# A linear-attention stage whose TensorE work is issued in the order of the program

## The chip, the core and the metric

The kernel runs on one core of a Trainium2 chip. The metric is the device time of one execution in microseconds (us). A core has a tensor engine for matrix products (TensorE, PE in the profile, with its weight loads as PEld), a vector engine (VectorE, DVE), a scalar engine (ScalarE, ACT), a general engine (GpSimd, POOL) and a queue engine (SyncE, SP) that mostly issues DMAs. Each engine takes its instructions in one fixed order; engines wait for each other through semaphores. Matrix products land in PSUM, a memory of eight banks; all else lives in SBUF.

## The reference

One inference step of a two-layer decoder, in float32: 512 new prompt tokens and 8 decode samples, model width 1024. Layer 0 mixes tokens with sliding-window attention, layer 1 with gated linear attention (GLA); after each comes an up-projection, a short convolution, a gate and a down-projection (ConvFFN, width 2816), and each sublayer ends in a LayerNorm of its sum with the input. The change lies in the GLA. For each of four heads:

```python
# log_a = log_sigmoid((x @ w_a1) @ w_a2 + b_a) / 16      rank-16 decay, from x
def step(S, inp):                       # one chunk of the sequence, state S is 128 x 256
    qc, kc, vc, lc = inp
    b = jnp.cumsum(lc, axis=2)
    q_in, k_in = qc * jnp.exp(b), kc * jnp.exp(-b)
    att = jnp.where(causal, q_in @ k_in.T, 0.0)
    o = att @ vc + q_in @ S
    S_new = exp(b_last) * S + (kc * jnp.exp(b_last - b)).T @ vc
o = o * rsqrt(mean(o ** 2) + eps) * norm_g * silu(g)     # then @ w_o
```

The eight samples do one such step each, from a state that is read from memory and written back.

## The kernel before

**Tiling.** Activations are kept transposed, 128 features by tokens, in two groups: a has 256 prompt tokens, b has 256 and the 8 samples. A weight matrix is cut into units of 128 output features. `plan` lists the units, `order` deals them out to the groups: within a phase (attention, out-projection, FFN, GLA, out-projection, FFN) group b follows group a by four or five units. The GLA phase has 25 units: the rank projection (`gla_rank`), and for each head q, k, v0, v1, g0, g1 (`gla_q`, `gla_k`, `gla_v`, `gla_g`).

**Main products.** `product` multiplies a unit with a group: float32 is split into a high and a low part, and each of eight slices takes three matmuls (L173 to L175), 24 in all, into one of four PSUM banks `accp`. The rank projection takes two per slice (L671, L672), 16 in all.

**Small products.** What is left are full float32 products and transposes: the decay of a head (L681), the scores k by q (L730), transposes of k and v (L750 to L752), the state update and the output (L767 `up`, L775 q by the scaled state `sp`, L778 the scores by v), the same for the samples (L814 to L816, then L827 and L828), and the transposes of the normed output for the gate (L866, L868). They use four more banks, by tag: two `sc`, one `tp`, one `pv` (`mtile`). A tile of a tag waits until the tag's earlier tile has been read.

**Order.** Each unit's work is a Python generator. `run` calls one unit per step, a slot; `yield n` puts the rest of the generator off by n slots, and `due` runs what is due after the unit's own product. The heap takes them by slot and then by the order in which they were put in. So in the program a unit's product comes first and the small products of earlier units behind it. The LayerNorm that ends the FFN of layer 0 is such a generator too (`ln_end`): for group b it resumes one slot after the last FFN unit, that is behind the rank projection of group a, with two sums over the features on PE (L256), then DVE, ACT and POOL steps that deliver eight chunks of 128 features (L296 to L301).

The program is not the order of issue. The framework (`TileContext`, with a timeline estimate) lists instructions that are ready, prefers those earlier in the program, and fixes an order for each engine when the kernel is built. It may issue a later product before an earlier one. `manual_schedule(engines=...)`, used at the kernel's start for SP alone (L323), keeps the named engines in program order for what is traced inside it.

**The samples.** `gla_sample` is started by group b's v1 unit. It transposes the samples' v, copies it to a DRAM tile and reads it back broadcast to 128 partitions; multiplies q with eight states (L827, 32 columns each); norms the result; and updates the states one pair per slot, with DVE and ACT operations pinned in program order (L844, L845).

Of the kernel before, what the change touches and what calls it, by code (L numbers as in the profile page):

```python
# [11 lines left out]
F32 = mybir.dt.float32  # L12
F32R = mybir.dt.float32r
I32 = mybir.dt.int32
AF = mybir.ActivationFunctionType
# [5 lines left out]
P = 128  # L21
# [70 lines left out]
class Net:  # L92
# [624 lines left out]
    def gla_k(self, g, u, h):  # L717
        nc, n = self.nc, g.n
        ps = self.product(g, u, g.xh, g.xl)
        yield 1  # L720
        g.k = self.gp.tile([P, n], F32, name=f"k_{g.name}")
        nc.vector.tensor_tensor(g.k, ps, g.em, op=ALU.mult)
        if g.i:
            g.kraw = self.gp.tile([P, NS], F32, name="kraw", bufs=2)
            nc.vector.tensor_copy(g.kraw, ps[:, 256:])
        yield 1
        att = self.mtile("sc")
        for b in range(2):
            bs = slice(b * P, (b + 1) * P)
            nc.tensor.matmul(att[:, bs], g.k[:, bs], g.q[:, bs], start=True, stop=True)  # L730
        g.att = self.attm[self.attm_i % 2]
        self.attm_i += 1
        nc.vector.copy_predicated(g.att, self.causal.unsqueeze(1).broadcast_to([P, 2, P]), att[:, :256].rearrange("p (b t) -> p b t", b=2))

    def gla_v(self, g, u, h, i):
        nc, n = self.nc, g.n
        ps = self.product(g, u, g.xh, g.xl)
        vt = self.gp.tile([P, n], F32, name=f"v{i}_{g.name}")
        nc.scalar.copy(vt, ps)
        if i == 0:  # L740
            g.v0 = vt
            return
        yield 1
        q, k, v0, v1, att, eb = g.q, g.k, g.v0, vt, g.att, g.eb
        ctx = dict(q=q, k=k, v0=v0, v1=v1, ep=g.ep, kraw=g.kraw) if g.i else None
        vks = []
        for b in range(2):
            bs = slice(b * P, (b + 1) * P)
            mp = self.mtile("tp")
            nc.tensor.transpose(mp[:, 0:P], k[:, bs], self.ident)  # L750
            nc.tensor.transpose(mp[:, P:2 * P], v0[:, bs], self.ident)
            nc.tensor.transpose(mp[:, 2 * P:3 * P], v1[:, bs], self.ident)  # L752
            vk = self.gp.tile([P, 3 * P], F32, name="vk", bufs=2)
            nc.scalar.copy(vk, mp[:, :3 * P])
            vks.append(vk)
        if g.i:
            self.spawn(self.gla_sample(g, h, **ctx), 0)
        yield 1
        o = self.mtile("pv")
        small = self.gp.tile([P, 8], F32, name="gsmall", bufs=2)  # L760
        st = self.tst[:, h]
        for b in range(2):
            bs = slice(b * P, (b + 1) * P)
            ob = o[:, b * 256:(b + 1) * 256]
            first = g.i == 0 and b == 0
            up = self.mtile("sc")[:, :256]
            nc.tensor.matmul(up, vks[b][:, 0:P], vks[b][:, P:], start=True, stop=True)  # L767
            if first:
                nc.vector.tensor_copy(st, up)
            else:  # L770
                f = self.gp.tile([P, 1], F32, name="f", bufs=2)
                nc.vector.tensor_tensor(f, self.ebl[:, h:h + 1], eb[:, 2 * b:2 * b + 1], op=ALU.mult)
                sp = self.gp.tile([P, 256], F32, name="sp", bufs=2)
                nc.vector.tensor_scalar(sp, st, f, None, op0=ALU.mult)
                nc.tensor.matmul(ob, q[:, bs], sp, start=True, stop=False)  # L775
                nc.vector.tensor_tensor(st, up, sp, op=ALU.add)
            nc.vector.tensor_copy(self.ebl[:, h:h + 1], eb[:, 2 * b + 1:2 * b + 2])
            nc.tensor.matmul(ob, att[:, b], vks[b][:, P:], start=first, stop=True)  # L778
        if g.i:
            so = self.gp.tile([P, 256], F32, name="sp", bufs=2)  # L780
            nc.vector.tensor_scalar(so, st, self.ebl[:, h:h + 1], None, op0=ALU.mult)
            nc.scalar.dma_start(out=self.O["gla_p"][h], in_=so)
        on = self.gp.tile([P, 512], F32, name="on", bufs=2)
        for b in range(2):
            ob = o[:, b * 256:(b + 1) * 256]
            nc.scalar.activation(on[:, b * 256:(b + 1) * 256], ob, AF.Square, accum_out=small[:, b:b + 1])
        rs = self.rms(small[:, 0:8], P, 2)
        for b in range(2):
            bs = slice(b * 256, (b + 1) * 256)
            nc.scalar.activation(on[:, bs], o[:, bs], AF.Copy, scale=rs[:, b:b + 1])  # L790
        g.on = on
# [13 lines left out]
    def gla_sample(self, g, h, q, k, v0, v1, ep, kraw):  # L805
# [22 lines left out]
        nc.tensor.matmul(os_, self.qkd, vs[:, :256], start=False, stop=True)  # L828
        small = self.gp.tile([P, 4], F32, name="ssmall")
        jk = self.gp.tile([P, 256], F32, name="sp", bufs=2)  # L830
        nc.scalar.activation(jk, os_, AF.Square, accum_out=small[:, 0:1])
        rs = self.rms(small, P, 1)
        g.os = self.gp.tile([P, 256], F32, name="osamp")
        nc.scalar.activation(g.os, os_, AF.Copy, scale=rs)
        yield SPAUSE if h < GH - 1 else SPAUSEL
        late = self.tc.keep_in_program_order
        for p in range(4):
# [14 lines left out]
    def gla_g(self, g, u, h, i):  # L852
        nc, n = self.nc, g.n
        if i == 0 and h < GH - 1:
            self.gla_decay(g, h + 1)
        ps = self.product(g, u, g.xh, g.xl)
        e = self.gp.tile([P, NT - 256], F32, name="de", bufs=1)[:, :n]
        nc.scalar.activation(e, ps, AF.Exp, scale=-1.0)
        nc.gpsimd.tensor_scalar(e, e, 1.0, 1.0, op0=ALU.mult, op1=ALU.add)
        nc.vector.reciprocal(e, e)  # L860
        sg = self.gp.tile([P, NT - 256], F32, name="sg", bufs=3)[:, :n]
        nc.vector.tensor_tensor(sg, ps, e, op=ALU.mult)
        yield 3 - i
        tp = self.mtile("tp")
        for b in range(2):
            nc.tensor.transpose(tp[:, b * P:(b + 1) * P], g.on[:, b * 256 + i * P:b * 256 + (i + 1) * P], self.ident)  # L866
        if g.i:
            nc.tensor.transpose(tp[:, 256:384], g.os[:, i * P:(i + 1) * P], self.ident)  # L868
        ng = self.par[:, C_NG + i:C_NG + i + 1]
        nc.vector.scalar_tensor_tensor(sg[:, :256], tp[:, :256], ng, sg[:, :256], op0=ALU.mult, op1=ALU.mult)  # L870
        if g.i:
            ss = sg[:, 256:].rearrange("p (t j) -> p t j", t=2)
            tps = tp[:, 256:384].rearrange("p (j s) -> p s j", j=4)[:, 0:2]
            nc.vector.scalar_tensor_tensor(ss, tps, ng, ss, op0=ALU.mult, op1=ALU.mult)
        c = 2 * h + i
        self.split(g.hh[:, c], g.hl[:, c], parted(sg))
# [83 lines left out]
    def run(self):  # L960
# [2 lines left out]
        self.nu, self.extra, self.close_wx = WSLOTS, {}, False  # L963
        self.attn_open()
        self.later, self.slot, self.seq, self.pool_mark = [], 0, 0, None
        for i, u in self.order():
            g = self.groups[i]
            _, _, f, a, pre = self.units[u]
            if i == 0 and pre:
# [134 lines left out]
```

## Time and profile before

| | us |
|---|---|
| median of 3 runs | 1149.12 (1148.29 to 1151.05) |
| the profiled execution | 1146.73 |
| its span, first to last instruction | 1144.7 |
| PE busy | 1104.2 (96% of the span) |
| DVE busy | 794.5 (69%) |
| ACT busy | 575.6 (50%) |
| POOL busy | 326.4 (29%) |

The profile's page gives busy time by engine, the chain of work that ended last, and groups of instructions by line, engine and tile. A timeline row gives start, length, engine, line, operation, output and inputs, and in brackets how long the engine idled before and what released it. A tile's number is left out of its name; `xs_a` is group a's split input, `xh_b` and `xl_b` are the high and low parts of group b's. An engine's matmul ends are modelled, so distances are taken from start to start. A full float32 product appears as two matmul records. The GLA stage lies between about 528 and 735 us of the span.

### The profile page before, as it was taken

The page shows a single profiled execution, that of the slowest core. Times are in us where ns is not written, and L with a number is a line of the kernel's source. Part 1 is how long each engine was busy: PE and PEld are TensorE (multiplying, and loading weights), DVE is VectorE, ACT ScalarE, POOL GpSimd, SP SyncE. Part 2 cuts the span into 40 slices and gives each one's busy share as a digit, 9 for nine tenths or more (in the row PEclk, how much of TensorE's full clock was granted, in tenths as well). Part 3 has the DMA queues.
Part 4 walks back from the last instruction along what each step waited for, and adds up shares of the span by engine and source line. Part 5 has one row for each costly group of instructions (what it writes and reads, how often), then busy time and mean ns, then how long its engine had stood idle before and what let it go on. Part 6 is the DMA issues. An engine that isn't in the chain of part 4 may idle for free.

```text
span 1144.7 us, 22953 instructions
## 1 busy us (share of the span) xinstructions
PE 1104.2 (96%) x8806; PEld 1055.2 (92%) x8806; DVE 794.5 (69%) x1663; ACT 575.6 (50%) x1253; POOL 326.4 (29%) x556
## 2 busy tenths in 40 slices
PE   8999899999999999999899999989999999999995
PEld 8997798999999999998899999888999999999994
DVE  7897589655665566668867777799655665566657
ACT  5677457534553245435545556456524553245433
POOL 4575568100110011357300101287100110011344
PEclk9999999999999999999899999999999999999998
DMA  7553031323323233243124355341333232232222
GB/s 241 149 183 90 13 111 56 111 93 123 99 93 111 92 99 105 74 133 110 38 89 147 117 177 162 133 145 62 105 96 127 93 106 98 92 111 93 74 63 75
DMA packets 53789, 122.82 MB, mean 107 GB/s; under 512 B 6792, under 2 KB 27312, under 8 KB 53680
## 3 DMA queue, kind: packets, MB, share of 16 engines
q1 hardware_dynamic: 51664, 119.61, 32.4%
q10 hardware_dynamic: 2016, 1.75, 0.5%
q8 instruction: 69, 1.13, 0.4%
q14 instruction: 40, 0.33, 0.1%
HBM read 108.67 MB, written 8.47 MB: 102 GB/s over the span
## 4 chain that ended last, share of the span: by engine, by line
PE 70%; DVE 12%; DMA 6%; ACT 4%; POOL 4%; issue 4%; SPq 0%; ACTq 0%; DVEq 0%; POOLq 0%
PE accp L191 15%; PE accp L174 14%; PE accp L173 14%; PE accp L175 14%; PE accp L192 8%; DMA vb<-dv 3%; DVE wl L161 2%; POOL x_b L298 1%; DVE sgla L845 1%; DMA qs<-hl 1%; ACT wh L158 1%; POOL x_a L298 1%; DVE u L296 1%; PE pv L494 1%; DVE msq L276 1%
## 5 line engine op out<-in xcount | busy, mean ns | idle before, releaser
L161 DVE TENSOR_TENSOR wl<-raw,wh 128x1024 fp32r<-128x1024 f32 (+2 forms) x189 | 231.4, 1226 | 106.7 <-ACT wh L158 105.2
L158 ACT ACTIVATE wh<-raw 128x1024 fp32r<-128x1024 f32 (+2 forms) x185 | 191.9, 1037 | 215.0 <-PE accp L174 196.8
L173 PE MATMUL accp<-xh_b,wh 128*128 128x264 f32 x976 | 271.7, 279 | 2.5 <-DVE hprod L600 2.5
L174 PE MATMUL accp<-xl_b,wh 128*128 128x264 f32 x976 | 271.3, 278 | 0.2
L175 PE MATMUL accp<-xh_b,wl 128*128 128x264 f32 x976 | 270.8, 278 | 0.0
L191 PE MATMUL accp<-xs_a,wh 128*128 128x512 f32 x576 | 196.3, 382 | 0.0
L173 PEld LDWEIGHTS accp<-xh_b,wh 128*128 128x128 f32 x976 | 185.0, 190 | 3.5 <-DVE hprod L600 2.9
L174 PEld LDWEIGHTS accp<-xl_b,wh 128*128 128x128 f32 x976 | 184.9, 189 | 3.1 <-DVE xl_b L301 0.6
L175 PEld LDWEIGHTS accp<-xh_b,wl 128*128 128x128 f32 x976 | 184.8, 189 | 0.8 <-issue 0.6
L192 PE MATMUL accp<-xs_a,wl 128*128 128x256 f32 x576 | 145.4, 273 | 0.0
L173 PE MATMUL accp<-hh_b,wh 128*128 128x264 f32 x480 | 133.7, 279 | 3.3 <-ACT hh_b L198 3.3
L174 PE MATMUL accp<-hl_b,wh 128*128 128x264 f32 x480 | 134.3, 280 | 0.0
L175 PE MATMUL accp<-hh_b,wl 128*128 128x264 f32 x480 | 133.3, 278 | 0.0
L191 PEld LDWEIGHTS accp<-xs_a,wh 128*128 128x128 f32 x576 | 109.1, 189 | 11.4
L173 PE MATMUL accp<-xs_a,wh 128*128 128x256 f32 x400 | 112.3, 287 | 5.6 <-DVE x_b L219 2.1
L174 PE MATMUL accp<-xs_a,wh 128*128 128x256 f32 x400 | 112.4, 283 | 3.2 <-DVE xs_a L301 2.9
L192 PEld LDWEIGHTS accp<-xs_a,wl 128*128 128x128 f32 x576 | 110.2, 191 | 1.9
L175 PE MATMUL accp<-xs_a,wl 128*128 128x256 f32 x400 | 111.0, 280 | 0.7 <-DVE wl L161 0.5
L173 PEld LDWEIGHTS accp<-hh_b,wh 128*128 128x128 f32 x480 | 91.3, 190 | 3.8 <-ACT hh_b L198 3.6
L174 PEld LDWEIGHTS accp<-hl_b,wh 128*128 128x128 f32 x480 | 91.3, 190 | 1.4 <-issue 0.3
L175 PEld LDWEIGHTS accp<-hh_b,wl 128*128 128x128 f32 x480 | 91.3, 190 | 0.2
L202 POOL COPY hist<-aext 128x2 f32<-128x2 f32 x44 | 8.9, 203 | 284.4 <-DVE aext L578 281.3
(320 smaller groups left out, 2495.3 us busy)
## 6 DMA issues: line engine op xcount, KB each, us to landing
raw<-in_w_up SPq DMA_DIRECT2D x88, 512.0 KB, 3.4
raw<-in_w_down SPq DMA_DIRECT2D x32, 512.0 KB, 3.4
raw<-in_w_gla SPq DMA_DIRECT2D x24, 512.0 KB, 3.4
raw<-in_w_mix_o SPq DMA_DIRECT2D x16, 512.0 KB, 4.1
raw<-in_w_down SPq DMA_DIRECT2D x16, 384.0 KB, 3.1
qs<-hl SPq DMA_DIRECT2D x64, 64.0 KB, 2.1
sgla<-in_state_gla SPq DMA_DIRECT2D x16, 256.0 KB, 2.8
vb<-dv SPq DMA_DIRECT2D x16, 256.0 KB, 3.7
```

The lines of the kernel that those rows point to most:

```text
L158: nc.scalar.activation(h[:, c], r[:, c], AF.Copy)
L161: nc.vector.tensor_tensor(l[:, c], r[:, c], h[:, c].bitcast(F32), op=ALU.subtract)
L173: nc.tensor.matmul(o, h[:, ks], xh, start=k == 0, stop=False)
L174: nc.tensor.matmul(o, h[:, ks], xl, start=False, stop=False)
L175: nc.tensor.matmul(o, l[:, ks], xh, start=False, stop=k == nt - 1)
L191: both = lambda: nc.tensor.matmul(o, h[:, ks], in_turn(rs[:, k].rearrange("p t q j -> p t (q j)")), start=k == 0, stop=last)
L192: low = lambda: nc.tensor.matmul(o[:, :P], l[:, ks], in_turn(rh[:, k]), start=False, stop=False)
L276: nc.vector.scalar_tensor_tensor(q, q, 0.5, nv, op0=ALU.mult, op1=ALU.mult)
L296: nc.vector.tensor_tensor(u, x[:, m], r, op=ALU.mult)
L298: ts = nc.gpsimd.tensor_scalar(x[:, m], u, sc(m), bi(m), op0=ALU.mult, op1=ALU.add)
L494: mm = nc.tensor.matmul(pv[64 * v:64 * v + 64, b * P:(b + 1) * P], self.vtok[:, kb, 64 * v:64 * v + 64], parts[v][w][:, b], start=i == 0, ...
L845: late(nc.vector.scalar_tensor_tensor(s[:, j], vb[:, j], kraw[:, b:b + 1], s[:, j], op0=ALU.mult, op1=ALU.add))
```

## The change

A region of program order is opened on PE at the first GLA unit and closed at the first unit of the out-projection behind it. In it, PE issues in the order in which the program traces. Besides:

- The scores go to the bank `pv` in place of `sc`; every second set of transposes (k and v of the second block, gate transposes of g1) goes to `sc` in place of `tp`.
- In the state update, the scores-by-v product stands ahead of q by state, so that the accumulation opens with the one and closes with the other.
- The samples start one slot later.
- The samples' output is copied to SBUF first (one ACT copy more), and squared and scaled from there.
- The gate transposes of g0 come four slots after their product in place of three, so that those of g0 and g1 fall in the same slot.

```diff
@@ gla_k
-        att = self.mtile("sc")
+        att = self.mtile("pv")
@@ gla_v
-            mp = self.mtile("tp")
+            mp = self.mtile("sc" if b else "tp")
...
-            self.spawn(self.gla_sample(g, h, **ctx), 0)
+            self.spawn(self.gla_sample(g, h, **ctx), 1)
...
             nc.tensor.matmul(up, vks[b][:, 0:P], vks[b][:, P:], start=True, stop=True)
+            nc.tensor.matmul(ob, att[:, b], vks[b][:, P:], start=True, stop=first)
...
-                nc.tensor.matmul(ob, q[:, bs], sp, start=True, stop=False)
+                nc.tensor.matmul(ob, q[:, bs], sp, start=False, stop=True)
                 nc.vector.tensor_tensor(st, up, sp, op=ALU.add)
             nc.vector.tensor_copy(self.ebl[:, h:h + 1], eb[:, 2 * b + 1:2 * b + 2])
-            nc.tensor.matmul(ob, att[:, b], vks[b][:, P:], start=first, stop=True)
@@ gla_sample
-        nc.scalar.activation(jk, os_, AF.Square, accum_out=small[:, 0:1])
+        g.os = self.gp.tile([P, 256], F32, name="osamp")
+        nc.scalar.copy(g.os, os_)
+        nc.scalar.activation(jk, g.os, AF.Square, accum_out=small[:, 0:1])
         rs = self.rms(small, P, 1)
-        g.os = self.gp.tile([P, 256], F32, name="osamp")
-        nc.scalar.activation(g.os, os_, AF.Copy, scale=rs)
+        nc.scalar.activation(g.os, g.os, AF.Copy, scale=rs)
@@ gla_g
-        yield 3 - i
-        tp = self.mtile("tp")
+        yield 4 - 2 * i
+        tp = self.mtile("sc" if i else "tp")
@@ run
+        region = ExitStack()
         for i, u in self.order():
+            if (i, u) == (0, self.phases[3]):
+                region.enter_context(self.tc.manual_schedule(engines={mybir.EngineType.PE}))
+            elif (i, u) == (0, self.phases[4]):
+                region.close()
```

## The prediction

> **What bounds the kernel now.** I read the page's head and its chain of waits first, then the busy times of the stretches that hold the linear-attention stage, then the timelines of VectorE (DVE), GpSimd (POOL) and TensorE (PE) there.
>
> ```profile
> span 1144.7 us, 22953 instructions
> PE 1104.2 (96%) x8806; PEld 1055.2 (92%) x8806; DVE 794.5 (69%) x1663; ACT 575.6 (50%) x1253; POOL 326.4 (29%) x556
> ...
> PE 70%; DVE 12%; DMA 6%; ACT 4%; POOL 4%; issue 4%; SPq 0%; ACTq 0%; DVEq 0%; POOLq 0%
> ```
>
> PE sets the time: 96% busy, and 70% of the chain that ended last. A change to PE's order can win only where PE now waits or runs slowly, and loses wherever a product stands in front of others and is not ready. The stage lies from about 528 to 735 us (columns: length; busy PE, PEld, DVE, ACT, POOL; clock; DMA share):
>
> ```profile
> 528.00:541.00 13.00, 10.51 (x86) 9.82 (x85) 12.16 (x27) 8.51 (x15) 11.46 (x9) 1.00 0.38 123
> 549.80:555.80 6.00, 3.92 (x17) 2.62 (x17) 5.61 (x18) 3.63 (x8) 4.17 (x4) 0.78 0.01 1
> 555.80:560.00 4.20, 4.20 (x18) 3.91 (x19) 1.95 (x3) 2.48 (x5) 0.00 (x0) 0.51 0.12 24
> 560.00:735.00 175.00, 173.62 (x1453) 164.54 (x1452) 131.36 (x314) 92.66 (x243) 18.75 (x25) 1.00 0.42 136
> 760.00:790.00 30.00, 24.99 (x208) 23.71 (x207) 29.55 (x56) 18.31 (x33) 25.63 (x26) 1.00 0.31 102
> ```
>
> So there are two parts. From 528 to 560 us DVE is the bound: 12.16 of 13 us, later 5.61 of 6, because the LayerNorm that ends the FFN before delivers its chunks one by one. From 560 to 735 PE is full: it idles 175.00 - 173.62 = 1.4 us. The clock stands at 0.51 for the 4.2 us after the thin stretch.
>
> **The change part by part. First the start of the stage.** These are the DVE and POOL rows of the LayerNorm chunks (the first and last of eight for each half), and PE's rows around them:
>
> ```profile
> 529.88 0.42 DVE L301 TENSOR_TENSOR xs_a<-x_a,xs_a 128x256 fp32r<-128x256 f32 x1 [0.46 <-POOL x_a L298]
> ...
> 540.40 0.96 DVE L301 TENSOR_TENSOR xs_a<-x_a,xs_a 128x256 fp32r<-128x256 f32 x1 [0.37 <-POOL x_a L298]
> ...
> 545.23 0.77 DVE L296 TENSOR_TENSOR u<-x_b,r 128x264 f32<-128x264 f32 x2
> ...
> 554.46 0.43 DVE L301 TENSOR_TENSOR xl_b<-x_b,xh_b 128x264 fp32r<-128x264 f32 x1
> ```
>
> ```profile
> 528.63 0.27 PE L671 MATMUL accp<-xs_a,wh 128*128 128x256 f32 x1
> ...
> 530.36 0.38 PE L672 MATMUL accp<-xs_a,wh 128*128 128x256 f32 x1 [1.35 <-DVE xs_a L301]
> ...
> 537.16 0.71 PE L256 MATMUL tp<-s_b,ones_a 128*128 128x264 f32 x2
> ...
> 549.76 0.38 PE L671 MATMUL accp<-xh_b,wh 128*128 128x264 f32 x1 [1.13 <-ACT v_a L739]
> ...
> 555.77 1.22 PE L730 MATMUL sc<-q_a,k_a 128*128 128x128 f32 x4 [0.23 <-DVE k_a L722]
> ...
> 558.71 0.43 PE L173 MATMUL accp<-xh_b,wh 128*128 128x264 f32 x1
> ```
>
> Today the scheduler fills the gaps between chunks: with each chunk it issues the two products of the rank projection (L671, L672) and also those of the q, k and v products (86 matmuls from 528 to 541). In program order the rank projection of group a stands first and alone: 16 products that each need a chunk. PE can go no further before the last chunk, 540.40 + 0.96 = 541.4. Behind it wait the LayerNorm sums of group b (L256, today at 537.16), then q, k, v0, v1, a decay product, the score products, a second decay product, gate product g0, the six transposes and group b's rank projection. Their prices:
>
> ```profile
> 581.76 0.27 PE L173 MATMUL accp<-xs_a,wh 128*128 128x256 f32 x1
> ...
> 584.44 0.27 PE L750 MATMUL tp<-ident,k_b 128*128 128x128 f32 x1
> ...
> 584.65 0.61 PE L730 MATMUL sc<-q_a,k_a 128*128 128x128 f32 x4
> 585.10 0.61 PE L681 MATMUL sc<-z_b,wa 128*128 128x264 f32 x2
> 585.55 0.27 PE L752 MATMUL tp<-ident,v_b 128*128 128x128 f32 x1
> ...
> 588.79 0.27 PE L750 MATMUL tp<-ident,k_b 128*128 128x128 f32 x1
> ...
> 589.12 0.60 PE L767 MATMUL sc<-vk 128*128 128x256 f32 x2
> 589.55 0.59 PE L778 MATMUL pv<-vk,attm 128*128 128x256 f32 x2
> ```
>
> By starts, 24 main matmuls take 584.44 - 581.76 = 2.68 us (0.112 each), the score or a decay product 0.45, three transposes 0.33, a 256-column small product 0.43. From 541.5: sums 2 x 0.45, four products 10.7, decay 0.45, scores 0.45, decay 0.45, g0 2.7, six transposes 0.66, rank b 1.8: 18.1 us, so 559.6. At 558.71 today all of that is done but three transposes, and two products of the next unit more: equal ground is 559.6 - 0.33 + 0.22 = 559.5, or **+0.8**. The clock: a stretch with 17 matmuls in 6 us ended at 0.51 for 4.2 us. Rank a alone is 16 matmuls in 13 us, so I expect the same 4.2 x 0.49 = 2.1 us after 541.5, while the 1.3 us at half clock that today still follow 558.71 (0.65) go: **+1.45**. Start: **+2.2**.
>
> [...]
>
> Bounds. The scores need k of group a, which needs the decay, whose DVE steps queue with group b's LayerNorm. Today k came just before 555.77. In the new order the scores' turn comes at 541.5 + 0.9 + 10.7 + 0.45 + 2.1 = 555.7, so no wait if DVE is no later. But the sums of group b move from 537.16 to 541.5; if all that follows moves too, the scores wait 4.3 us, and g0 and rank b queue behind them. DVE chunks of b began only at 545.23, after POOL had subtracted the mean, and the decay can use DVE before that, so I take 0 and keep 0 to +6.5 for the start as a whole (not below: the chunk rate, not PE, sets 541.4).
>
> **The full part.** What PE waits for from 560 to 735, and the 32-column products of the decode sample (L827), once unbroken and once split:
>
> ```profile
> PE tp L750 <- DVE sg L870: 0.8, 2, 0.6
> PE tp L866 <- ACT on L790: 0.4, 1, 0.4
> PE sc L827 <- DVE tst L776: 0.2, 1, 0.2
> ```
>
> ```profile
> 593.62 1.07 PE L827 MATMUL sc<-sgla,qz 128*32 128x256 f32 x16
> ...
> 594.83 0.28 PE L173 MATMUL accp<-xh_b,wh 128*128 128x264 f32 x1
> ```
>
> ```profile
> 640.04 0.64 PE L827 MATMUL sc<-sgla,qz 128*32 128x256 f32 x8
> ...
> 642.46 0.59 PE L828 MATMUL sc<-vsamp,qkd 128*128 128x256 f32 x2
> ```
>
> The second bank for the transposes, the later g0 transposes (four slots after the product instead of three) and the score bank moved from "sc" to "pv" are aimed at such waits: all three together are 1.4 us. Gathering itself: around a small group the starts add up to the groups' own prices, as 584.44 to 585.55 show (two transposes 0.22, scores 0.45, decay 0.45: 1.11 us, 1.12 worked out), so switching between main and small products costs nothing I can see. Only the split sample costs: 2.42 us less two pairs (0.86) against 1.21 unbroken, 0.35 each; two of four heads show it. Gain at most 1.4 + 0.7, and I take **-2.1** (bounds 0 and -2.1).
>
> Against it stands the state update. Per head and group PE now issues up, att, q·sp, up, att, q·sp in one piece, and the last one waits for DVE: L776 (state), L777, L772 and L774.
>
> ```profile
> L161 DVE TENSOR_TENSOR wl<-raw,wh 128x1024 fp32r<-128x1024 f32 x24 | 29.4, 1224 | 4.3 <-ACT wh L158 3.9 <-PE accp L175 0.3
> L860 DVE RECIPROCAL de<-de 128x256 f32<-128x256 f32 (+1 forms) x16 | 28.4, 1774 | 1.7 <-POOL de L859 1.7
> ...
> L776 DVE TENSOR_TENSOR tst<-sc,sp 128x256 f32<-128x256 f32 x12 | 4.9, 409 | 0.0
> ...
> L774 DVE TENSOR_SCALAR sp<-tst,f 128x256 f32<-128x256 f32 x12 | 4.0, 334 | 0.1
> ```
>
> Between the first up and the last q·sp stand att, q·sp, up and att: 4 x 0.43 = 1.72 us of cover. The chain is 0.41 + 0.33 and two one-column steps that I estimate at 0.3 together, near 1.05: 0.65 to spare. But DVE is 75% busy, a third of the time (57.8 of 175 us) with casts of 1.22 us or reciprocals of 1.77 us, and a gate product, whose reciprocal follows, stands right ahead of seven of the eight updates. Without wait 0; with one reciprocal in the chain each time 8 x (1.77 - 0.65) = 9. Half a long operation is left on average (0.75), in a third of cases, with shorter ones besides: 0.2 each, **+1.6**, nearer to 0 since the scheduler that orders DVE sees the chain.
>
> Parts that I cost at nothing. The sample's output is now copied to SBUF before it is squared, one more ACT copy per head; a like one takes 0.37 us, and ACT is 92.66 of 175 us busy; uncovered it is 4 x 0.37 = 1.5. The sample starts one slot later, and with it, per head, one store, four broadcast loads, four state stores and up to four state loads on SP's queue pass one weight load; DVE, whose state updates wait for those broadcasts, shows what lateness means there:
>
> ```profile
> L739 ACT COPY v_b<-accp 128x264 f32<-128x264 f32 x8 | 2.9, 365 | 0.0
> ...
> DVE sgla L845 <- DMA vb<-dv: 15.4, 8, 2.8
> ```
>
> Those waits are as long after the move, and their loads for the next head are needed six units (16 us) on. The last g0 transposes come two units before the out-projection of group b, cover 5.4 us. If this cover failed, one 2.8 us wait would reach PE.
>
> Sum: 2.2 - 2.1 + 1.6 = **+1.7 us**. The profiled execution took 1146.73 us (span 1144.7); it would become 1148.4. That execution lies 2.4 below the median of 1149.12, so I put the difference on the median: **1150.8 us**.
>
> **Rivals.** (1) The update decides: if a reciprocal stands in the chain at each of the eight updates, PE waits 1.1 us there. It decides the sign from 0.45 us each on. +2.2 - 2.1 + 9 = +9.1: 1158.2. For it: the gate product right ahead; against: 0.65 us to spare. (2) The start decides: the scores wait the whole 4.3 us: +6.0, 1155.1. For it: DVE 5.61 of 6 us; against: the decay's earlier place. [...] (5) The order scarcely differs from today's inside the stage: 1149.1. Against it: the interleaved chunks at its start.
>
> **How the numbers follow.** A measurement of this kernel can tell about 0.3%, 3.4 us: 1145.7 to 1152.6 counts as no change. Chances: the forecast 0.36 (its own range 1147.5 to 1152.6), (1) 0.17, (2) 0.13, (3) 0.08, (4) 0.21, (5) 0.05. Faster is (4), 0.21; the same is the forecast, (3) and (5), 0.49; slower is (1) and (2), 0.30. The range takes (1) and (4) in with the bounds of the unknown costs around them: 1142.5 to 1159.
>
> **What would show it.** Start: L671 and L672 of group a alone on PE until near 541, the sums L256 right after, a clock near 0.5 then, and rank b after g0; wrong if main products still run between the chunks. Full part: L827 in one run of 16 per head, no PE wait for L870 or L790; and for the update, PE waiting at L775 for DVE's L774. The forecast is wrong if the stretch from 560 to the stage's end changes by over 4 us, or if the start loses over 5.

## The result, and the profile after

The changed kernel takes 1168.16 us (median of 4 runs, 1166.64 to 1172.59) against 1149.14 us (1148.29 to 1151.05): ratio 1.0173, 95% interval 1.0154 to 1.0192. It is 19 us slower. The forecast was 1150.8 us, its range ended at 1159: it was wrong in size, and the likeliest case (no change) did not come.

The head of the page and its chain of waits, changed kernel:

```profile
span 1170.9 us, 22968 instructions
PE 1114.4 (95%) x8806; PEld 1062.1 (91%) x8806; DVE 795.8 (68%) x1663; ACT 578.8 (49%) x1257; POOL 318.1 (27%) x556
...
PE 69%; DVE 12%; DMA 5%; POOL 5%; issue 5%; ACT 3%; SPq 0%; ACTq 0%; DVEq 0%; POOLq 0%
```

The work is the same: 8806 matmuls, and DVE is busy for 795.8 us in place of 794.5. What is new is time in which PE stands or runs at a low clock. To place it I compare the moment at which the n-th matmul starts in the two traces (after less before, us):

| n-th matmul (its time before) | changed kernel | what lies between |
|---|---|---|
| 1186 (149.9) | +2.2 | unchanged code of the attention stage |
| 4118 (528.1) | +2.1 | nothing |
| 4294 (559.2) | +10.5 | start of the GLA stage: **+8.4** |
| 5749 (735.0) | +21.2 | its four heads: **+10.7** |
| 6022 (770.1) | +26.2 | end of the last head, out-projection: **+5.0** |
| 8718 (1120.1) | +26.2 | nothing |

The profiled executions are the kernel's slowest of four (1172.59) and, for before, one below its median (1146.73), so the places add up to more than the 19 us between the medians; 2.1 of it lies in code that nobody changed, where the clock stood at half for 6.8 us in place of 3.4 (1.7 us of the 2.1).

**The start.** Stretches of the changed kernel (length; busy PE, PEld, DVE, ACT, POOL; clock; DMA):

```profile
528.00:543.40 15.40, 8.33 (x43) 6.37 (x42) 13.71 (x30) 8.03 (x13) 10.60 (x8) 0.75 0.41 137
543.40:556.70 13.30, 13.30 (x103) 12.78 (x102) 10.57 (x22) 7.07 (x15) 9.07 (x11) 0.90 0.00 1
556.70:560.50 3.80, 0.17 (x3) 0.03 (x1) 3.69 (x14) 2.29 (x6) 2.15 (x3) 0.88 0.01 2
560.50:567.60 7.10, 7.10 (x37) 6.92 (x37) 2.21 (x5) 1.83 (x5) 0.00 (x0) 0.58 0.01 2
567.60:740.00 172.40, 164.43 (x1349) 155.57 (x1347) 120.13 (x285) 89.71 (x221) 8.48 (x15) 0.99 0.40 130
```

Where 86 matmuls ran in 13 us before, 43 run in 15.4. Then comes a stretch of 3.8 us with three matmuls, and behind it 7.1 us at a clock of 0.58. What PE stood for, with the rows of PE and then of DVE at that place:

```profile
543.36 1.09 PE L256 MATMUL tp<-s_b,ones_a 128*128 128x264 f32 x2
...
556.56 0.28 PE L175 MATMUL accp<-xs_a,wl 128*128 128x256 f32 x1
560.47 1.22 PE L730 MATMUL pv<-q_a,k_a 128*128 128x128 f32 x4 [3.63 <-DVE k_a L722]
```

```profile
558.53 0.42 DVE L301 TENSOR_TENSOR xl_b<-x_b,xh_b 128x264 fp32r<-128x264 f32 x1
...
559.67 0.42 DVE L715 SCALAR_TENSOR_TENSOR q_a<-accp,ep 128x256 f32<-128x256 f32 x1
560.00 0.41 DVE L722 TENSOR_TENSOR k_a<-accp,em 128x256 f32<-128x256 f32 x1
```

The scores of group a come to their turn 3.63 us before DVE has made `k_a`, since DVE is busy with the LayerNorm chunks of group b.

**The heads.** What PE waited for from 530 to 760 us, changed kernel (us in total, times, longest):

```profile
PE accp L672 <- DVE xs_a L301: 7.1, 6, 2.2
PE pv L777 <- DVE sp L776: 5.0, 4, 2.2
PE pv L730 <- DVE k_a L722: 3.6, 1, 3.6
PE sc L828 <- DVE tst L778: 2.3, 1, 2.3
```

The new waits are those for the state update (L776, L778). One of them in full, DVE first:

```profile
687.80 0.88 DVE L847 SCALAR_TENSOR_TENSOR sgla<-vb,kraw,sgla 128x256 f32<-128x256 f32 x2 [3.55 <-DMA vb<-dv]
688.60 1.22 DVE L161 TENSOR_TENSOR wl<-raw,wh 128x1024 fp32r<-128x1024 f32 x1
689.74 0.44 DVE L733 COPY_PREDICATED attm<-causal,pv 128x256 f32<-128x256 int32 x1
...
692.10 0.43 DVE L689 TENSOR_TENSOR dmn<-dmn,de 128x264 f32<-128x264 f32 x1 [1.55 <-ACT de L688]
...
693.71 0.41 DVE L778 TENSOR_TENSOR tst<-sc,sp 128x256 f32<-128x256 f32 x1
...
694.17 1.21 DVE L161 TENSOR_TENSOR wl<-raw,wh 128x1024 fp32r<-128x1024 f32 x1
695.31 0.33 DVE L776 TENSOR_SCALAR sp<-tst,f 128x256 f32<-128x256 f32 x1
```

```profile
693.05 0.59 PE L769 MATMUL pv<-vk,attm 128*128 128x256 f32 x2
695.70 0.83 PE L777 MATMUL pv<-sp,q_b 128*128 128x256 f32 x2 [2.05 <-DVE sp L776]
```

DVE stood 3.55 us at a state update of the samples (L847), until the broadcast `vb` had landed, with all else queued behind it. It then owed a cast, the mask of the scores, the decay (1.55 us for ACT) and only then the state; a second cast stood inside the update chain. PE, which may take no other product, stood 2.05 us.

Before, a wait of this kind stood in the same place, right ahead of the mask, and cost PE nothing. An update in the kernel before, DVE first (line numbers are one or two lower there: L774 makes `sp`, L775 uses it):

```profile
630.48 0.88 DVE L845 SCALAR_TENSOR_TENSOR sgla<-vb,kraw,sgla 128x256 f32<-128x256 f32 x2 [2.40 <-DMA vb<-dv]
...
631.67 0.44 DVE L733 COPY_PREDICATED attm<-causal,sc 128x256 f32<-128x256 int32 x1
...
639.32 0.34 DVE L774 TENSOR_SCALAR sp<-tst,f 128x256 f32<-128x256 f32 x1
```

```profile
638.63 0.70 PE L767 MATMUL sc<-vk 128*128 128x256 f32 x2
638.98 0.46 PE L173 MATMUL accp<-xh_b,wh 128*128 128x264 f32 x1
...
640.61 0.70 PE L775 MATMUL pv<-sp,q_b 128*128 128x256 f32 x2
```

From the end of the wait to the finished `sp` DVE took 9.2 us there, more than the 7.8 us of the changed kernel's rows. But between the update's product L767 and L775, which needs `sp`, PE had seven main matmuls and eight of the sample's, and came to L775 at 640.61, when `sp` had been done since 639.66. Those eight are the first half of the split L827, which the prediction counted as a loss of 0.35 us: here it is part of the cover.

Two groups of DVE's waits from 569 to 765 us, changed kernel (for the broadcasts, and for ACT's Square of the samples' output):

```profile
DVE sgla L847 <- DMA vb<-dv: 21.0, 9, 3.7
DVE ssmall L798 <- ACT sp L834: 11.2, 4, 4.1
```

Before, the first was 15.4 us, 2.8 at the longest, and the second was no more than 0.8.

### The profile page after: what moved, and what is told of

It reads as the page before. It is cut to its first block, busy times and chain, and to the rows that moved or that the text cites. A ratio compares the mean times of both kernels' runs of the same rounds, so it can differ in the third digit from the quotient of the medians.

```text
span 1170.9 us, 22968 instructions
## 1 busy us (share of the span) xinstructions
PE 1114.4 (95%) x8806; PEld 1062.1 (91%) x8806; DVE 795.8 (68%) x1663; ACT 578.8 (49%) x1257; POOL 318.1 (27%) x556
## 4 chain that ended last, share of the span: by engine, by line
PE 69%; DVE 12%; DMA 5%; POOL 5%; issue 5%; ACT 3%; SPq 0%; ACTq 0%; DVEq 0%; POOLq 0%
PE accp L191 15%; PE accp L174 14%; PE accp L175 14%; PE accp L173 14%; PE accp L192 7%; DMA vb<-dv 3%; DVE wl L161 2%; POOL x_b L298 1%; DMA raw<-in_w_qkv 1%; POOL x_a L298 1%; POOL x_a L232 1%; DVE sgla L847 1%; PE pv L494 1%; DMA qs<-hl 1%; DVE msq L276 1%
```

## The experiments

All are compared with runs of the kernel before on the same chip, whose median lay between 1148.6 and 1149.5 us. "Progress" is the difference of the n-th matmul's start, as above. What the expectations call the planner is the framework's ordering of instructions when the kernel is built; the region or fixed order is `manual_schedule` on PE.

### The region without the other edits

```diff
 # kernel before, and in run():
+ the five lines that open and close the region
```

> The kernel before with the region of program order alone; banks, order of the products in the update, pauses and the samples' copy stay as before. Theory O (the order itself costs, at the start of the stage and at the updates, and the other edits soften it): at least the 19 us of the whole change are lost, since here the product q by state stands ahead of scores by v and has one product less (0.43 us) of cover at each of 15 places: 1168 to 1180 us. Rival E (the other edits carry the loss, most of all the later samples and the score bank pv): 1149 to 1155 us.

Measured: 1176.0 us (1175.01 to 1178.27), ratio 1.0238 (1.0217 to 1.0259). PE's largest wait:

```profile
PE tp L750 <- ACT vk L754: 9.3, 8, 3.0
```

The fixed order is what costs; the banks and slots are made for it and win some 8 us back (26.5 us lost here, 19.0 with them): the second set of transposes no longer waits for the first set's bank (9.3 us).

### The edits without the region

```diff
 # changed kernel, run():
- the five lines that open and close the region
```

> The changed kernel without the region: the scheduler orders PE as before, all other edits stand. Theory O: within 3 us of before, 1146 to 1153 us. Rival E: 1160 us or more, with PE waits at the product q by state also here.

Measured: 1155.14 us (1153.6 to 1156.03), ratio 1.0052 (1.0036 to 1.0069), between the two expectations. Progress is +1.4 at matmul 5548 (710 us) and +9.1 at 6022: 1.4 us of it were lost ahead of the stage, all the rest at the end of the last head. PE's two largest waits from 690 us on:

```profile
PE tp L256 <- DVE s_a L247: 2.3, 1, 2.3
PE sc L828 <- DMA sgla<-in_state_gla: 2.2, 1, 2.2
```

### The region begun six units later

```diff
-            if (i, u) == (0, self.phases[3]):
+            if (i, u) == (0, self.phases[3] + 6):
```

> The changed kernel with the region opened six units later, behind the rank projection of group b, so that PE's order is the scheduler's while the LayerNorm chunks arrive. Theory S (the start is the largest single part: PE alone with the rank projection until 543 us, then 3.6 us of waiting for k, then a low clock, in the profiles +8.5 us of the difference between equal points of the program): 1168.2 - 8.5 = 1159.7 us. Rival U (the updates and the end of the stage carry it; time won at the start is lost again because DVE, not PE, sets the pace there): 1166 us or more.

Six units on, group a is at the last unit of its first head (g1) and group b is through with its rank projection; group b's first head still lies in the region. (Where later expectations say "in the second head", this place is meant.)

Measured: 1165.52 us (1164.63 to 1167.85), ratio 1.0147 (1.0129 to 1.0165): 3.0 us back (16.0 lost in place of 19.0), where the trace puts 8.4 at the start. The start is free indeed (progress -0.1 at matmul 4294), but the heads now cost +13.5 up to 5749 and the end +4.3. The waits that stayed are those at the update:

```profile
PE pv L777 <- DVE sp L776: 5.1, 4, 2.3
...
PE sc L828 <- DVE tst L778: 2.0, 1, 2.0
```

So the start is a loss of its own, and something else, in the heads, is at least as large.

### The last q·sp product one slot later

```diff
-                nc.tensor.matmul(ob, q[:, bs], sp, start=False, stop=True)
+                if b == 0:
+                    nc.tensor.matmul(ob, q[:, bs], sp, start=False, stop=True)
                 nc.vector.tensor_tensor(st, up, sp, op=ALU.add)
...
+            if b:
+                yield 1
+                nc.tensor.matmul(ob, q[:, bs], sp, start=False, stop=True)
```

> The changed kernel with the last product q by state of each update put off by one slot, behind one more main product (2.7 us of cover); the scaled states get one buffer each in place of two in turn. Theory U: the waits of PE at that product (5.0 us in the profile, 2.2 us the longest) and the low clock that follows the longest go: 1168.2 - 5.0 - 1.5 = 1161.7 us, and the profile shows no PE wait for the scaled state. Rival (DVE is late as a whole, and the wait moves to the next product that needs it): 1166 us or more, with the waits under another line.

Measured: 1175.23 us (1171.39 to 1178.09), ratio 1.0226 (1.02 to 1.0252). The wait for `sp` is gone, and PE waits for the output's norm instead:

```profile
PE tp L872 <- ACT on L795: 6.4, 2, 3.3
```

The norm comes behind the product that was put off, so it is a slot later too: the wait moved down the chain, and the time did not come back. That fits DVE and ACT being late as a whole, but this run alone doesn't show it. From here the theory (V) was that DVE's own stream, held up by the broadcasts, is what PE in fixed order waits for.

### One broadcast for four

```diff
+        vb = self.gp.tile([P, 2, 256], F32, name="vb")
+        nc.sync.dma_start(out=vb, in_=dv[0:2].unsqueeze(0).broadcast_to([P, 2, 256]))
         yield SPAUSE if h < GH - 1 else SPAUSEL
...
-            vb = self.gp.tile([P, 2, 256], F32, name="vb")
-            nc.sync.dma_start(out=vb, in_=dv[2 * p:2 * p + 2].unsqueeze(0).broadcast_to([P, 2, 256]))
             yield 1
```

> The changed kernel with three of the four broadcasts of sample values left out in each head: one is loaded, ahead of the pause, and serves all four state updates (the samples' new state is then that of the first pair's values, so it isn't the reference's; every other instruction stays). VectorE then never stands behind a broadcast: in the changed kernel it stood 21.0 us so, 9 times, 3.7 us at the longest, with the casts and the chain of the q·sp products behind it. Theory V (VectorE's stream, held up by these transfers, is what TensorE in fixed order waits for): the loss between 560 and 760 us of the traces, 16 us in the changed kernel against the kernel before, falls to 8 or less, so 1156 to 1161 us. Rival W (VectorE comes late for the update whatever stands ahead of it, since the casts are placed between the two updates): no more than 3 us less, 1165 to 1169 us.

Measured: 1157.39 us (1154.17 to 1159.11), ratio 1.0067 (1.0043 to 1.0091): 10.8 us back, as theory V has it. Progress between matmul 4294 and 5749 is +1.0 in place of +10.7, and +1.4 in place of +5.0 at the end; the start stays (+8.3). PE's wait at the update, and DVE's rows at one:

```profile
PE pv L777 <- DVE sp L776: 1.7, 4, 0.5
```

```profile
640.64 0.45 DVE L733 COPY_PREDICATED attm<-causal,pv 128x256 f32<-128x256 int32 x1 [1.57 <-PE pv L730]
...
644.76 0.42 DVE L778 TENSOR_TENSOR tst<-sc,sp 128x256 f32<-128x256 f32 x1
...
645.43 1.21 DVE L161 TENSOR_TENSOR wl<-raw,wh 128x1024 fp32r<-128x1024 f32 x1
646.57 0.34 DVE L776 TENSOR_SCALAR sp<-tst,f 128x256 f32<-128x256 f32 x1
```

The cast still stands between L778 and L776. DVE now waits for the scores (1.57 us for PE), where it was the other way about, and the cast's 1.21 us cost PE 0.5 at most at one update, 1.7 at four. Rival W, that the cast in the chain is enough, falls. (To leave transfers out gives the planner another picture too, but these rows stand in the same order as in the changed kernel's fence above, and PE's sequence is that of the changed kernel up to 737 us.)

### The state updates not pinned

```diff
-                late(nc.scalar.activation(s[:, j], s[:, j], AF.Copy, scale=ep[:, 256 + b:257 + b]))
-                late(nc.vector.scalar_tensor_tensor(s[:, j], vb[:, j], kraw[:, b:b + 1], s[:, j], op0=ALU.mult, op1=ALU.add))
+                nc.scalar.activation(s[:, j], s[:, j], AF.Copy, scale=ep[:, 256 + b:257 + b])
+                nc.vector.scalar_tensor_tensor(s[:, j], vb[:, j], kraw[:, b:b + 1], s[:, j], op0=ALU.mult, op1=ALU.add)
```

> The changed kernel with the samples' state updates no longer pinned to the place in the program's order (the planner may put other work of VectorE and ScalarE ahead of them). Theory V: the planner lets casts and update chains past the updates that wait for a broadcast, 1157 to 1163 us. Rival: the planner's times show no wait there and it places them as before, or the state loads of the next head come late in their place and the sample products wait: 1166 us or more.

Measured: 1178.0 us (1176.85 to 1178.75), ratio 1.0249 (1.0231 to 1.0267). The planner placed them worse: DVE's wait for broadcasts grew (from 560 to 770 us, with 21.6 us in the changed kernel), and PE's with it.

```profile
PE pv L777 <- DVE sp L776: 9.8, 6, 5.4
```

```profile
DVE sgla L847 <- DMA vb<-dv: 25.9, 11, 4.8
```

This fits theory V in the other direction, more blocking and more time, but the fix that I expected of it failed.

### The sample begun at once

```diff
-            self.spawn(self.gla_sample(g, h, **ctx), 1)
+            self.spawn(self.gla_sample(g, h, **ctx), 0)
```

> The changed kernel with the sample's small products begun one slot earlier, as before the change (that edit alone undone). Theory S (the later sample pushes the broadcasts, the state updates and the loads of the next head's state a slot back, and this is most of the 5.7 us which the edits cost without the region): 1162 to 1164 us. Theory V says nothing of it: the broadcasts' waits stay and move a slot, 1166 to 1170 us.

Measured: 1162.96 us (1161.24 to 1164.09), ratio 1.0114 (1.0092 to 1.0136): 5.2 us back. DVE waits for the broadcasts as long as in the changed kernel (21.6 us there too from 569 to 770 us), but PE no longer stands at the update:

```profile
DVE sgla L847 <- DMA vb<-dv: 21.6, 12, 3.1
```

```profile
PE accp L175 <- DVE wl L161: 3.4, 4, 2.2
PE tp L815 <- ACT vk L754: 3.0, 1, 3.0
...
PE pv L777 <- DVE sp L776: 0.2, 1, 0.2
```

Progress over the heads is +1.0 from matmul 4294 to 5548, then +7.2 within 10 us in the last head, where the transposes wait 3.0 us for ACT and the clock then stands at half for 6.8 us (3.4 us more). DVE at the update of the second head:

```profile
637.90 0.88 DVE L847 SCALAR_TENSOR_TENSOR sgla<-vb,kraw,sgla 128x256 f32<-128x256 f32 x2 [2.28 <-DMA vb<-dv]
...
643.61 0.40 DVE L778 TENSOR_TENSOR tst<-sc,sp 128x256 f32<-128x256 f32 x1
...
644.05 0.35 DVE L776 TENSOR_SCALAR sp<-tst,f 128x256 f32<-128x256 f32 x1
```

A wait still stands right ahead of the mask, decay and state, but it is 2.28 us long, where the changed kernel has 3.71 at the same update, and no cast stands between L778 and L776. So the total of the broadcasts' waits doesn't decide, but how much of it stands ahead of what PE needs next; the cast's place has a part in it, and no run tells the two shares apart. Theory V as I put it for this run (no change) was too narrow. Theory S named the right edit, and its 1162 to 1164 us was met, but by luck: its reason, that this edit is most of what the edits cost without the region, falls with the next run.

### The edits without the region, the sample at once

The same line as above, in the kernel with all edits and no region.

> All edits without the region, but the sample begun one slot earlier as before. Theory S: the 5.7 us of the edits are gone, 1148.5 to 1151 us, and in its profile the wait of the last sample products for the loaded state (2.2 us) and the half clock behind it are gone. Rival (another of the edits, the banks or the transposes' slot): 1153 to 1156 us.

Measured: 1155.56 us (1154.89 to 1156.04), ratio 1.0054 (1.0037 to 1.0072). Without the region the slot of the sample is worth nothing. The four runs together: with the sample late the region costs 13.3 us (19.0 against 5.7 without it), with the sample at once 7.4 (13.8 against 6.4), and of those 7.4 the trace puts 7.3 at the start of the stage. The loss is at the end of the last head again (progress +3.0 at matmul 5628, +9.5 at 6022). A suspect there is ACT's Square, which stood for a buffer that a DMA was still reading:

```profile
730.06 0.42 ACT L834 ACTIVATE sp<-osamp 128x256 f32<-128x256 f32 x1 [3.06 <-DMA out_gla_p<-sp]
```

### Late region and sample at once

Both edits together in the changed kernel, nothing left out of the computation.

> The changed kernel with the fixed order begun six units later (in the second head) and the sample begun one slot earlier, as before the change: two parts undone together, the computation whole. Theory V with S (the loss at the start is a matter of the few first units, and the middle of the stage costs nothing once the sample's transfers keep their old place): the sample at once alone gave 1163.0 us, of which 8.3 lie ahead of 560 us, so 1154 to 1157 us. Rival (the planner's new picture gives the gain at the start back later, as when the fixed order began later with the sample late): 1160 us or more.

Measured: 1157.52 us (1156.07 to 1160.21), ratio 1.0079 (1.0057 to 1.0101), half a us above what theory V gave. It is 8.9 us above the kernel before, of which the edits have 6.4 without any region. The start is even, the heads cost +3.4 up to matmul 5548, and +6.3 follows in the last head, where PE waits 3.8 us for ACT's copy `vk` and the clock stands at half for 6.8 us.

### Late region and one broadcast

The edit of the region's start and that of the broadcasts, together.

> The changed kernel with the fixed order begun six units later and one broadcast of sample values for each head in place of four (so the samples' new state isn't the reference's). Theory V adds: 1157.4 us with one broadcast, of which 8.3 at the start, so 1148 to 1151 us. Rival (no adding: the planner places other work worse once the start is free): 1154 us or more.

Measured: 1150.93 us (10 runs, 1149.67 to 1155.48), ratio 1.0023 (1.001 to 1.0036). Of 19.0 us, 16.7 are gone: the forecast was met at its upper end. Singly the two edits took away 3.0 and 10.8 us, so the late region is worth more once the broadcasts are out, though not the 8.3 us that the trace puts at the start.

### Controls: one broadcast in the kernel before, and with the edits alone

> The control to the two runs with one broadcast: the kernel before, with three of the four broadcasts of sample values left out in each head and nothing else changed. If in the planner's order VectorE's waits for broadcasts (15.4 us in the kernel before) cover nothing that TensorE needs, 1147.5 to 1150 us, and the 10.8 us that one broadcast gave in the changed kernel belong to the fixed order. Rival (the broadcasts cost this kernel too): 1145 us or less, or, since each single edit so far cost 5 to 8 us at the end of the stage through a new plan, 1153 us or more.

Measured: 1148.32 us (10 runs, 1145.94 to 1149.43), ratio 0.9996 (0.9985 to 1.0007). Nothing. In the planner's order 15.4 us of DVE's waits were free, and the 10.8 us belong to the fixed order. (Leaving transfers out gave the planner another order here, so a gain and a loss that cancel are not excluded.)

> The same control to the edits without the fixed order (1155.1 us): if their loss at the end of the last head is the late broadcasts that hold VectorE ahead of weight casts, 1148 to 1151 us. Rival (the loss there is of the plan as a whole, with another wait in each variant): 1153 us or more.

Measured: 1151.16 us (10 runs, 1149.58 to 1153.67), ratio 1.0018 (1.0008 to 1.0029), on the edge of the first expectation. Of the 5.7 us of the edits alone 3.3 are the broadcasts too. And with them out, the edits with the late region (+2.3 us) and without it (+2.3) are the same: the fixed order from the seventh unit on has neither gain nor cost left.

### What in the edits costs the rest

Four runs, each without the region: the copy undone (beside the sample at once), the Square into the products' own bank, and single edits on the kernel before.

```diff
 # the copy undone
-        nc.scalar.copy(g.os, os_)
-        nc.scalar.activation(jk, g.os, AF.Square, accum_out=small[:, 0:1])
+        nc.scalar.activation(jk, os_, AF.Square, accum_out=small[:, 0:1])
...
-        nc.scalar.activation(g.os, g.os, AF.Copy, scale=rs)
+        nc.scalar.activation(g.os, os_, AF.Copy, scale=rs)
 # the Square into the bank
-        nc.scalar.activation(jk, g.os, AF.Square, accum_out=small[:, 0:1])
+        nc.scalar.activation(os_, g.os, AF.Square, accum_out=small[:, 0:1])
```

> All edits without the fixed order, the sample at once, and the samples' output squared and scaled straight from its bank as before (the copy ahead of it left out): what is left of the change are the banks, the place of the q·sp products and the slot of the transposes. Theory C (the copy makes ScalarE's chain longer, VectorE stood 3.8 us at its end behind the Square, and this is most of the 6.4 us by which the edits with the sample at once are slower): 1149 to 1151.5 us. Rival (the slot of the last transposes or the banks): 1153.5 to 1156.5 us.

Measured: 1156.3 us (1155.56 to 1160.02), ratio 1.0072 (1.0049 to 1.0096). Without the region the copy costs nothing.

> All edits without the fixed order, the sample at once, and the square of the samples' output written back into the bank of the products (which the copy has read) in place of one of the two buffers sp. In the run of the edits with the sample at once, ScalarE's Square of the last head stood 3.06 us for that buffer until the state's output transfer had read it, and VectorE 3.84 us behind it; the whole loss of that run lay behind this place. Theory B (that buffer): the 6.4 us are gone, 1148.5 to 1151 us. Rival (the Square is late for another reason, or the loss at the end of the stage comes from the late broadcasts of the last head alone): 1153.5 to 1157 us.

Measured: 1153.77 us (1151.39 to 1154.92), ratio 1.0037 (1.0024 to 1.005). The cost falls from 6.4 us in its sister to 4.6, the rival's number: the buffer is a part of it, some 1.8 us. The two traces have the same order of instructions on PE, DVE and ACT, so a new plan has no share in this difference.

The three single edits, each as in the diff of the change: the order of the two products in the state update, the transposes' slot and bank, and the banks of scores and of the second set of transposes.

> The kernel before with one edit: the product of scores and values ahead of the q·sp product in their shared bank (the accumulation begins with the one that doesn't wait for sp). It lets go of the values earlier and has q·sp as last; without the fixed order the planner could place either. Theory: no change, 1148 to 1150.5 us, at best 1 us less. Rival (this edit carries the 6 us of the edits): 1153 us or more.

> The kernel before with one edit: the transposes of the normalized output for both halves of the gate at one slot (the first one later by a slot) and in two kinds of banks. Theory T (the first half's output of the last head is a slot later, and the output projection behind it stands with it): 1152 to 1156 us. Rival (no part in it): 1148 to 1150.5 us.

> The kernel before with the banks alone changed: the scores take the bank of the head's output, and the transposes of keys and values of the second half take a bank of the other kind. Theory: no change, 1148 to 1150.5 us; the waits of those transposes for the copy are in the kernel before under 1 us in all. Rival (the banks carry the 6 us): 1153 us or more.

Measured: 1157.28 us (1156.71 to 1157.91; ratio 1.0068, 1.0053 to 1.0083), 1155.24 us (1154.33 to 1156.95; 1.0052, 1.0037 to 1.0067) and 1153.74 us (1152.86 to 1155.42; 1.0042, 1.0027 to 1.0056). The two forecasts of "no change" fail. The transposes met the number of theory T, but as the others cost as much, their slot is nothing special. The three costs (8.1, 6.1, 4.6 us) add up to 18.8, three times what all edits with the sample at once cost (6.4). They have no common wait, only a common place: progress from matmul 5548 to 6022 (710 to 770 us) is +5.7, +7.6 and +6.3. I read this as the planner's order at the end of the stage: each edit makes it anew, and the kernel before has a better one there than each of these. That is argued, not shown. PE's sequence is indeed another one in all three (1038, 1174 and 1472 matmuls stand elsewhere, from the first or second head on), but it is as different in the kernel before with one broadcast (953), which lost nothing: a new order need not cost.

### The region for the middle heads alone

```diff
-            if (i, u) == (0, self.phases[3]):
+            if (i, u) == (0, self.phases[3] + 6):
...
-            elif (i, u) == (0, self.phases[4]):
+            elif (i, u) == (0, self.phases[3] + 19):
```

with the sample at once and the copy undone.

> The fixed order for the middle of the stage alone (from the second head to the start of the last one), the sample at once and the samples' output taken straight from its bank: all three places of loss that the traces show (the start, VectorE's waits for broadcasts, the last head) are left to the planner. Theory V: 1148 to 1151.5 us, the kernel before within its uncertainty. Rival (fixed order costs wherever it stands): 1154 us or more.

Measured: 1158.56 us (1157.76 to 1160.27), ratio 1.0088 (1.0066 to 1.011). The rival's number, but not for the rival's reason: the same edits without any region took 1156.3 us, 7.7 of these 10.0 us, so the fixed order itself adds 2.3 us, and the two runs' ranges overlap. Progress is +3.9 over the middle heads (matmul 4294 to 5296) and +6.0 from 5749 to 6022, behind the region's end, where the planner is on its own. No version found beats the kernel before.

## Why the prediction was wrong, point by point

| kernel | less the kernel before, us (medians) |
|---|---|
| changed | +19.0 |
| region begun six units later | +16.0 |
| one broadcast | +8.3 |
| late region and one broadcast | +2.3 |
| edits alone, one broadcast | +2.3 |

**The start, +2.2 forecast, +8.4 in the trace.** Its shape was right: group a's rank projection stands alone, the sums come right behind it at 543.36 (541.3 without the 2.1 us carried in; 541.4 forecast), the clock falls. The step that failed is "so no wait if DVE is no later", and the choice of 0 for it. DVE was later: `k_a` was done at 560.4, 2.6 us later than before if the 2.1 carried in are taken off. PE came to the scores a little earlier than forecast and stood 3.63 us. Rival 2 had this wait (4.3 us) and gave it the wrong price, for it left out what comes behind: 7.1 us at a clock of 0.58, which is 7.1 x 0.42 = 3.0 us. Forecast plus both is 2.2 + 3.6 + 3.0 = 8.8, against 8.4. The bound of +6.5 was too low by that second stretch. That the clock holds at the start, as case (3) of the chances and the faster case (4) have it, no run shows: it was 0.75 and 0.58 here, 0.70 (530 to 543 us) and 0.61 (560 to 567.6) in the run with one broadcast.

**The steady gain, -2.1 forecast, none found.** The waits that the banks were to remove are gone from PE's list, and L828 (L827 before) is one run of 16 in three heads of four. But with both causes of loss taken away, the kernel is no faster than the edits without the region. Waits of 1.4 us in all were replaced by others: 3.8 us from 562 to 740 us in the run with the late region and one broadcast. And the split of L827, counted as 0.7 us to be won, had been part of the cover of an update (640.04 us in the kernel before).

**The update waits, +1.6 forecast, the bulk of +10.7 in the trace.** PE's waits there and at the samples' products are 7.8 us (5.0, 2.3 and 0.5), and two stretches at half clock behind them, 3.4 us long, cost 1.7 each: 11.2 in all, which covers the +10.7. The mechanism was named (PE stands at q·sp for L776), and the wrong thing was varied: I asked which long operation could stand inside the chain of four DVE steps and gave it 0.65 us to spare. A cast did stand there; once DVE was on time PE's waits for `sp` came to 1.7 us, 0.5 at the longest, so for long operations in the chain the +1.6 was of the right size. What I didn't ask is whether DVE begins the chain on time.

**"Parts that I cost at nothing".** This is the step that decided. "Those waits are as long after the move" was wrong in size (15.4 to 21.0 us) and, which matters more, they were priced as if only their length counted. In DVE's stream a wait holds what is queued behind it: behind the 3.55 us at L847 stood a cast, the mask, the decay and the state. A broadcast's wait stands in front of mask, decay and state in both kernels; in the changed one it is 3.7 us there in place of 2.4, and where PE had other products to go on with in the planner's order, in fixed order it had none. If the cover failed I expected one wait of 2.8 us; PE stood at four of the updates, 5.0 us in all, and once at the samples' products (2.3), and twice the clock was at half for 3.4 us behind it. Taking the blocking away gave 10.8 us, moving it back one slot 5.2. The ACT copy in the same paragraph was rightly put at nothing, as far as the run without the region shows.

**The end of the stage, not in the sum.** +5.0 in the trace, some of it the broadcasts (+1.4 without them). I had looked at the g0 transposes alone there.

**What stays open.** The last 2.3 us, which the edits cost even without region and broadcasts, and why each single edit costs 4.6 to 8.1 us at the end of the stage. That the planner's order there is at fault is argued from the common place and the missing common wait; no run shows an order with all edits and that place as before, and one new order cost nothing.

## What to carry to other kernels

Putting one engine in program order takes away the cover that let the other engines be late at no cost, so before doing it, list the waits that stand in *their* streams, with what is queued behind each: in one order 15.4 us of VectorE's waits were free, in the other 21.0 us of such waits cost 10.8. An edit that moves blocking waits is to be priced by what stands behind each of them, not by their total. And where a framework orders the instructions, measure each edit alone against a rebuilt order: here three edits that looked like nothing cost 5 to 8 us each, most likely through the order that was found for them.

## What the runs showed of the hardware

Of two stands of PE in the changed kernel the shorter one cost twice, by the wait and by the clock behind it. PE stood at L777 once for 2.22 us and once for the 2.05 us shown above. The first, and the stretches right behind both:

```profile
649.44 0.70 PE L777 MATMUL pv<-sp,q_b 128*128 128x256 f32 x2 [2.22 <-DVE sp L776]
```

```profile
649.30:655.00 5.70, 5.56 (x51) 4.76 (x52) 3.59 (x13) 3.46 (x13) 0.00 (x0) 1.00 0.49 161
...
695.60:700.60 5.00, 4.90 (x26) 4.70 (x26) 3.54 (x13) 1.87 (x8) 0.00 (x0) 0.66 0.45 144
```

Behind the longer one the clock stayed at 1.00; behind the shorter one it was 0.66, and 24 main matmuls took 4.59 us in place of the 2.68 of the prediction's rows. So the length of a gap alone doesn't decide. In the traces of the kernel before and of the changed one the record of the granted clock is 1.00 or 0.50, and ahead of an execution's end its stretches at half last 3.41 us (four of them), 6.83 us (three) or 10.24 us (one). (The 0.66 above is half clock from 696.1 to 699.5 us, begun after PE was back at work at 695.70, and full clock around it.) What set the half clock behind the one gap and not behind the other, no run shows.
